# The last FFN of a hybrid block: instructions in a written order on every engine, two tiles ahead, and one more group in seven block products

## The chip, the cores and the metric

The kernel runs on one core of a Trainium2 chip. The metric is the device time of one execution in microseconds (us). Of the kernel before three runs were timed: 1880.12, 1881.79 and 1884.59, median 1881.79.

The engines are named as in the profile: PE is TensorE (matmul), DVE is VectorE, ACT is ScalarE, POOL is GpSimd and SP is SyncE, on which most DMAs are issued.

## The reference

One block over 256 tokens of 2048 channels, in float32: an FFN (SwiGLU), a mixer (mLSTM heads beside an RG-LRU), and a second FFN, each with a residual and a layer norm, and each modulated by shift, scale and gate that come from a vector c ("adaLN"). What matters here is the second, the last FFN:

```python
def _swiglu(u, w13, w2):
    g, v = jnp.split(u @ w13, 2, axis=-1)
    return (jax.nn.silu(g) * v) @ w2
...
mod = (jax.nn.silu(c) @ w_ada[l] + b_ada[l]).reshape(B, N_SUBLAYERS, 3, D_MODEL)
...
y = _swiglu(modulate(x, 2), ffn2_w13[l], ffn2_w2[l])
x = _layer_norm(ALPHA * x + FFN_WEIGHT * gate[:, 2, None, :] * y, ln_g[l, 2], ln_b[l, 2])
```

w13 is 2048 x 11264 (5632 gate columns g and 5632 value columns v), w2 is 5632 x 2048.

## The kernel before

**Products in halves.** Each float32 weight tile (128 x 2048, 1 MB) is loaded by a DMA on SP and split in two float32r halves: ACT casts the high half (`split`, L108), DVE subtracts it from the tile for the low half (L110). A product of a tile with 128 tokens is 12 matmuls of 512 columns: for each of four row blocks high by high, low weight by high, and high weight by low token half (`mov_t`). A tile that multiplies both token tiles (256 tokens) takes 24. Raw tiles have four buffers, high and low halves three each.

**Groups.** The last FFN goes through the 5632 columns in 11 groups of 512, called 0 to 10. For each group it makes g and v, then silu(g) * v as a 128 x 512 tile for each token tile, turns that by four transposes on PE (tile `th`, `turn_one`, L814), and ACT and DVE make its high and low half (`hth`, L816, and `htl`, L817). The w2 products of a pair of groups are added over the pair and then into `yacc` (L743, L745). Such a w2 product of one tile with both token tiles is called an X step below; the X steps of a pair run in the two groups behind it, four in each, two for a block of 512 output columns: the first with the pair's even group, the second with its odd one.

**Plain and fast groups.** Groups 0, 1 and 10 are plain (`rows_block`): eight tiles, 192 matmuls. Groups 2 to 9 are fast (`fast_block`): on half of the columns the 2 x 2 block product is done with seven block products in place of eight, P1 to P7 in the words of this text, each 12 matmuls, with sums of the weight tiles that DVE makes in place, and sums of the tokens (`sums`) that are made once. The other tiles of a fast group are two G (gate) and two V (value), 24 matmuls each. A fast group thus has 7 x 12 + 4 x 24 = 180 matmuls, and 4 x 24 = 96 with its X steps: 276. In the trace of before the seven products' tiles are `hfw`/`lfw`: P1 is the tile with b0 (`lfw_50` in group 5), P5 `50p` (its weight is a subtraction at L756), P6 `50q` (L761), P3 `55`, P7 `54q` (L766), P2 `51`, P4 `51p` (L775). The banks are `fa` (P1, then P6 and P7), `fb` (P5 and P3), `fc` and `fd`. ACT copies each product out (`kept`, L730); DVE adds the finished sums (L780, L782, L792) and multiplies (L793).

**adaLN tiles.** Shift, scale and gate need one DVE instruction for each 1 MB tile of w_ada (`ada_tile`, L210). 16 of them, those for the last gate, are left when the last FFN begins; before, `tick` gives one for every second load.

**Ahead and behind.** Before group 2 the residual x is written to DRAM (tile `xd`), its place is used for the token sums, and `restore` reads it back behind group 9 (`x<-xd`, POOL) and scales it. `closing` does the X steps of the last three groups, called (n, k) for output block n and group 8 + k; `residual` (L334, L335) adds what is finished to x. The last block of columns has its weight tiles multiplied by the gate first (`gated`, L1035), and `boundary` ends the kernel with the residual and the layer norm.

**What sets the order.** PE's matmuls, and where `V`, `A`, `G`, `T` or `Q` stands in place of `nc.vector` and so on, are issued in the program's order on their engine ("pinned"). In the last FFN before only PE's matmuls are pinned; the splits, sums, copies, turns and additions on DVE and ACT, and the loads, are placed by a scheduler.

## Time and profile before

| | us |
|---|---|
| profiled execution | 1882.46 |
| its span, first to last instruction | 1880.7 |
| PE busy | 1861.4 |
| DVE busy | 1561.3 |
| ACT busy | 895.1 |
| POOL busy | 43.2 |
| last FFN, from about 1177 to the end | 703.7 |

The mean granted clock of TensorE is 0.998 of full speed. In the rows below a line begins with its start and its length in us (timeline), or with its line, engine, operation, output and inputs (groups); the number in brackets is the idle time of the engine ahead of it, and what ended it. Records of matmuls overlap: the distance of their starts is what one costs.

### The profile page before, as it was taken

The numbers are of one execution on the slowest core, as the hardware profiler recorded it, in microseconds if no ns is written. First come the engines' busy times: TensorE is split into PE (matmuls) and PEld (weight loads), VectorE is DVE, ScalarE is ACT, GpSimd is POOL, SyncE is SP. The second block draws the span as 40 slices with busy tenths as digits, with TensorE's granted clock in tenths as the row PEclk, the third lists the DMA queues.
The fourth block names the chain that finished last, engine by engine and source line by source line (L and its number), as shares of the span: only waits on it lengthen the run. The fifth ranks groups of instructions, "written<-read, shape, count | busy, mean of one in ns | idle before, by whom it ended". The sixth has DMA issues, their size and how long they took to land.

```text
span 1880.7 us, 21240 instructions
## 1 busy us (share of the span) xinstructions
PE 1861.4 (99%) x8495; PEld 1526.0 (81%) x8495; DVE 1561.3 (83%) x1467; ACT 895.1 (48%) x847; POOL 43.2 (2%) x68
## 2 busy tenths in 40 slices
PE   8999999999999999999999999999999999999998
PEld 5788888888888888788888887878778888888886
DVE  6899998887887987889997877789887788778776
ACT  4543444533334335756644356454544455545441
POOL 0000000000000000100000121000000000000000
PEclk9999999999999999999999999999999999999999
DMA  9989889999899987478687574768855654564662
GB/s 377 417 354 366 319 311 347 357 348 355 344 357 355 339 331 269 148 276 296 244 317 296 203 264 182 268 246 300 307 210 190 224 212 168 202 224 186 239 224 90
DMA packets 74931, 520.06 MB, mean 277 GB/s; under 512 B 8736, under 2 KB 8912, under 8 KB 13520
## 3 DMA queue, kind: packets, MB, share of 16 engines
q1 hardware_dynamic: 72144, 507.54, 71.6%
q0 software_dynamic: 960, 7.37, 1.0%
q10 hardware_dynamic: 1728, 3.80, 0.6%
q8 instruction: 66, 1.08, 0.2%
q14 instruction: 33, 0.27, 0.0%
HBM read 514.46 MB, written 4.22 MB: 276 GB/s over the span
## 4 chain that ended last, share of the span: by engine, by line
PE 92%; DVE 4%; DMA 2%; issue 1%; ACT 1%; POOL 0%; POOLq 0%; DVEq 0%; SPq 0%; ACTq 0%
PE py L133 9%; PE pj L281 5%; PE fa L133 5%; PE fb L133 4%; PE fc L133 3%; PE fd L133 3%; PE py L293 3%; PE py L294 3%; PE py L292 3%; PE pj L283 3%; PE fg L293 3%; PE fg L294 3%; PE fg L292 3%; PE fv L293 3%; PE fv L292 3%; PE fv L294 3%
## 5 line engine op out<-in xcount | busy, mean ns | idle before, releaser
L210 DVE CUSTOM_DVE_ANT_0 ada<-ada,scb,badac 128x2048 f32<-128x2048 f32 x110 | 258.0, 2345 | 39.5 <-DMA ada<-in_w_ada 39.0
L108 ACT CAST hw<-rw 128x2048 fp32r<-128x2048 f32 x81 | 155.1, 1914 | 218.0 <-DMA rw<-in_w 60.6
L110 DVE TENSOR_TENSOR lw<-rw,hw 128x2048 fp32r<-128x2048 f32 x81 | 185.1, 2287 | 55.8 <-ACT hw L108 55.0
L110 DVE TENSOR_TENSOR lfw<-rfw,hfw 128x2048 fp32r<-128x2048 f32 x48 | 109.9, 2289 | 17.2 <-ACT hfw L108 17.2
L281 PE MATMUL pj<-u,hs 128*128 128x512 f32 x512 | 122.5, 391 | 0.0
L108 ACT CAST hra<-rra 128x2048 fp32r<-128x2048 f32 x38 | 72.6, 1914 | 102.2 <-DMA rra<-in_w_r 43.1
L108 ACT CAST hfw<-rfw 128x2048 fp32r<-128x2048 f32 x48 | 91.9, 1915 | 47.8 <-PE py L133 28.2
L281 PEld LDWEIGHTS pj<-u,hs 128*128 128x128 f32 x512 | 94.3, 188 | 18.4
L133 PE MATMUL py<-lw,hth 128*128 128x512 f32 x256 | 99.8, 390 | 2.1 <-DVE lw L110 2.1
L133 PE MATMUL py<-hw,hth 128*128 128x512 f32 x256 | 100.4, 392 | 0.0
L293 PE MATMUL py<-lw,hth 128*128 128x512 f32 x256 | 99.8, 390 | 0.1
L294 PE MATMUL py<-hw,htl 128*128 128x512 f32 x256 | 99.7, 390 | 0.0
L133 PE MATMUL py<-hw,htl 128*128 128x512 f32 x256 | 99.7, 389 | 0.0
L292 PE MATMUL py<-hw,hth 128*128 128x512 f32 x256 | 97.3, 392 | 0.0
L108 ACT CAST hfg<-rfg 128x2048 fp32r<-128x2048 f32 x28 | 53.6, 1914 | 86.1 <-DMA rfg<-in_w 48.8
L108 ACT CAST hs<-rs 128x2048 fp32r<-128x2048 f32 x32 | 61.0, 1908 | 68.7 <-PE pj L281 53.6
L293 PE MATMUL fg<-lfg,u 128*128 128x512 f32 x224 | 87.4, 390 | 0.1
L294 PE MATMUL fg<-hfg,u 128*128 128x512 f32 x224 | 87.3, 390 | 0.0
L293 PE MATMUL fv<-lfv,u 128*128 128x512 f32 x224 | 87.2, 389 | 0.0
L294 PE MATMUL fv<-hfv,u 128*128 128x512 f32 x224 | 87.1, 389 | 0.0
L108 ACT CAST hfv<-rfv 128x2048 fp32r<-128x2048 f32 x28 | 53.6, 1913 | 66.7 <-DMA rfv<-in_w 41.3
L292 PE MATMUL fg<-hfg,u 128*128 128x512 f32 x224 | 84.5, 392 | 0.0
(727 smaller groups left out, 4764.4 us busy)
## 6 DMA issues: line engine op xcount, KB each, us to landing
ada<-in_w_ada SPq DMA_DIRECT2D x138, 1024.0 KB, 6.5
rw<-in_w SPq DMA_DIRECT2D x81, 1024.0 KB, 5.5
rfw<-in_w SPq DMA_DIRECT2D x50, 1024.0 KB, 4.8
rra<-in_w_r SPq DMA_DIRECT2D x45, 1024.0 KB, 7.4
rs<-in_w_s SPq DMA_DIRECT2D x32, 1024.0 KB, 5.0
rfg<-in_w SPq DMA_DIRECT2D x28, 1024.0 KB, 6.7
rfv<-in_w SPq DMA_DIRECT2D x28, 1024.0 KB, 5.5
rwo<-in_w_out SPq DMA_DIRECT2D x16, 1024.0 KB, 4.8
```

Of the source, the lines that this page charges most:

```text
L108: act.copy(cut(hi, w), like(raw[:, w], hi))
L110: low.tensor_sub(cut(lo, w), like(raw[:, w], lo), cut(hi, w).bitcast(F32))
L133: self.last = getattr(self.engine, op)(*args, **kw)
L210: vec.tensor_tensor_reduce(raw[:, c], raw[:, c], scb[:, c], 1.0, base, ALU.mult, ALU.add, to)
L281: nc.tensor.matmul(ps, hi[:, k * P:(k + 1) * P], both(k), start=k == 0, stop=False)
L283: nc.tensor.matmul(ps[:, 0:S], lo[:, k * P:(k + 1) * P], uh[:, k, :], start=False, stop=k == KT - 1)
L292: pe.matmul(o, acth[:, k0 + j, tk], cut(hi, w), start=first and j == 0, stop=False, **kw)
L293: pe.matmul(o, acth[:, k0 + j, tk], cut(lo, w), start=False, stop=False, **kw)
L294: end = pe.matmul(o, actl[:, k0 + j, tk], cut(hi, w), start=False, stop=last and j == 3, **kw)
```

## The change

A new function `last_ffn` takes the place of the branches in `ffn` that made the last FFN. It first writes a list of steps (a PE part, a preparation of its weight, and work behind it), and then issues them (`flow`), everything pinned: weight tiles are prepared as long as no more than AHEAD = 3 prepared tiles are held, the current one among them; the work behind a step is issued right behind its matmuls, and the products that some steps return ahead of the next preparations. `beside` places extra work behind given preparations: seven adaLN tiles, the scaling of x, its DMA to DRAM and the token sums in groups 0 and 1, and nine adaLN tiles behind every third preparation in groups 2 and 3.

The order of a group is a string: `P` and `G`/`V` as above, `X` an X step and `t` a turn. Groups 2 to 9 use S4, and group 10, which is now fast too, uses S2 with two of the closing's steps in it.

The residual isn't read back: `gated_sum` multiplies `yacc` by the gate (two times four 512-wide products behind two preparations of group 10), and a DMA on POOL adds the scaled x from DRAM into it. The gate's row is fetched four preparations ahead of group 10. P6's weight is made with a scalar_tensor_tensor, its sign turned, so that P4's is an addition. `gated` for the closing's first tile comes behind all its steps.

The core of the diff:

```diff
-    ffn(2, a["w13_2"], a["w2_2"], None)
+    last_ffn(2, a["w13_2"], a["w2_2"])
...
+AHEAD = 3
+S4 = "P1 t X t P5 X P6 P3 X P7 P2 G P4 G X V V"
+S2 = "P1 t G t P5 X P6 P3 G P7 P2 X P4 V V"
...
+        def flow():
+
+            hls, late, n, m = {}, [], 0, 0
+            for i, (pe, prep, after) in enumerate(steps):
+                for f in late:
+                    f()
+                while n < len(steps) and (n <= i or len(hls) < AHEAD):
+                    if steps[n][1]:
+                        hls[n] = steps[n][1]()
+                        for f in extras.get(m, ()):
+                            f()
+                        m += 1
+                    n += 1
+                pe(hls.pop(i, None))
+                late = after() or [] if after else []
...
+            def after():
+                b, t, ps = now.pop()
...
+                A.copy(hth[:, :, tk], ps)
+                V.tensor_sub(htl[:, :, tk], ps, hth[:, :, tk].bitcast(F32))
...
+                if w == "P5":
+                    W["c", q] = raw(q, 4, row_c)
+                    a, c = W["a", q], W["c", q]
+                    V.tensor_sub(a[0], c[0], a[0])
+                    hl = halves(a, "p")
...
+                if w == "P6":
+                    W["d", q] = raw(q, 5, q == 1)
+                    a, d = W["a", q], W["d", q]
+                    V.scalar_tensor_tensor(a[0], a[0], -1.0, d[0], op0=ALU.mult, op1=ALU.subtract)
+                    hl = halves(a, "q")
...
+        def gated_sum(t):
+            def go():
+                for n in range(4):
+                    c = slice(n * 512, (n + 1) * 512)
+                    V.tensor_mul(yacc[t][:, c], yacc[t][:, c], gate[:, c])
+                G.dma_start(yacc[t], xd[:, t, :], accum_op=ALU.add)
...
+        beside([scaled(0), scaled(1), ada, ada, ada, *sums(0, in_x), ada, ada])
+        first_group(nxt.pop())
+        plain_group(1)
+        beside([ada] * 9, 3, 3)
+        for b in range(2, n_b - 1, 2):
...
+                for i in range(2):
+                    fast_group(b + i, 1, xs, S4, b > 2 and not DOUBLE)
...
+        beside([lambda: gate_rows(s, 0.5)], -4)
+        beside([gated_sum(0), gated_sum(1)], 4, 2)
...
+            for n, k in ((0, 0), (0, 1), (1, 0), (1, 1), (0, 2), (1, 2), (2, 0), (2, 1), (2, 2)):
...
+        flow()
+        fine[0] = True
+        gated(0)
```

Where it moves instructions. DVE at the head of group 6, before: `lfw_60p` and `lfw_60q` are the low halves for P5 and P6, L756 and L761 the subtractions that make their weights, `lw_4_0` and `lw_5_0` the low halves of the X steps, `htl` the low halves of the turned tokens, L792 and L793 the former group's last additions and products.

```order
L110 TENSOR_TENSOR lfw_60_10592<-fw_10589,hfw_60_10591 128x2048
L756 TENSOR_TENSOR fw_10589<-fw_10616,fw_10589 128x2048
L792 TENSOR_TENSOR fv_10321<-fv_10321,fb_10182 128x512
L766 TENSOR_TENSOR fw_10616<-rfw_65_10676,fw_10616 128x2048
L793 TENSOR_TENSOR fs_10208<-fs_10208,fv_10321 128x512
L110 TENSOR_TENSOR lw_4_0_10623<-rw_4_0_10620,hw_4_0_10622 128x2048
L792 TENSOR_TENSOR ft_10268<-ft_10268,fa_10181 128x512
L110 TENSOR_TENSOR lfw_60p<-fw_10589,hfw_60p 128x2048
```

The same place on DVE now; every pinned instruction has one line number, that of the helper that issues it. `f_...` are the sums of the products, `ht` the turned tokens.

```order
L142 TENSOR_TENSOR f_10332<-f_10332,f_10269 128x512
L142 TENSOR_TENSOR f_10282<-f_10282,f_10200 128x512
L142 TENSOR_TENSOR f_10213<-f_10213,f_10332 128x512
L142 TENSOR_TENSOR f_10401<-f_10401,f_10282 128x512
L142 TENSOR_TENSOR fw_60_10536<-fw_64_10600,fw_60_10536 128x2048
L142 TENSOR_TENSOR lfw_60p<-fw_60_10536,hfw_60p 128x2048
L142 TENSOR_TENSOR lw_5_0_10625<-rw_5_0_10622,hw_5_0_10624 128x2048
L142 TENSOR_TENSOR ht_10628<-th_10629,ht_10628 128x4x128
L142 SCALAR_TENSOR_TENSOR fw_60_10536<-fw_60_10536,rfw_65_10662 128x2048
L142 TENSOR_TENSOR lfw_60q<-fw_60_10536,hfw_60q 128x2048
L142 TENSOR_TENSOR ht_10628<-th_10669,ht_10628 128x4x128
```

The subtraction for P5 has moved from ahead of the former group's last additions to behind them and both products. The scalar_tensor_tensor for P6 stands between the two turns' low halves, and the second of these behind `lfw_60q`.

ACT at the same place, before: `hfw_60q` is P6's high half, `hth` the high half of the turned tokens.

```order
L108 CAST hfw_60p<-fw_10589 128x2048
L108 CAST hw_5_0_10680<-rw_5_0_10678 128x2048
L816 CAST hth_10175<-th_10607 128x4x128
L730 COPY fs_10614<-fa_10587 128x512
L816 CAST hth_10175<-th_10650 128x4x128
L108 CAST hfw_60q<-fw_10589 128x2048
L730 COPY ft_10674<-fb_10588 128x512
```

And now:

```order
L142 CAST hfw_60p<-fw_60_10536 128x2048
L142 COPY f_10620<-f_10607 128x512
L142 CAST hw_5_0_10624<-rw_5_0_10622 128x2048
L142 CAST ht_10628<-th_10629 128x4x128
L142 CAST hfw_60q<-fw_60_10536 128x2048
L142 CAST ht_10628<-th_10669 128x4x128
L142 COPY f_10689<-f_10676 128x512
```

The cast of the second turn (`ht_...<-th_...`, its second row) has moved behind the cast of `hfw_60q`.

DVE in the middle of group 3, with the adaLN tiles (ISA rows), now; `lfw_30q` is P6's low half, `lfw_34q` P7's, and the rows ahead of them make their weights.

```order
L142 ISA ada_9395,adac<-ada_9395,scb,badac 128x2048
L142 ISA adac 128x1
L142 TENSOR_TENSOR ht_9398<-th_9399,ht_9398 128x4x128
L142 SCALAR_TENSOR_TENSOR fw_30_9300<-fw_30_9300,rfw_35_9432 128x2048
L142 TENSOR_TENSOR lfw_30q<-fw_30_9300,hfw_30q 128x2048
L142 TENSOR_TENSOR ht_9398<-th_9439,ht_9398 128x4x128
L142 TENSOR_TENSOR lfw_35_9462<-rfw_35_9432,hfw_35_9461 128x2048
L142 TENSOR_TENSOR lw_0_3_9494<-rw_0_3_9491,hw_0_3_9493 128x2048
L142 ISA ada_9497,adac<-ada_9497,scb,badac 128x2048
L142 ISA adac 128x1
L142 TENSOR_TENSOR rfw_34_9367<-rfw_34_9367,rfw_35_9432 128x2048
L142 TENSOR_TENSOR lfw_34q<-rfw_34_9367,hfw_34q 128x2048
```

Before, the scheduler placed such tiles, as in group 2 ahead of `lfw_20q`:

```order
L761 TENSOR_TENSOR fw_8922<-rfw_25_9015,fw_8922 128x2048
L817 TENSOR_TENSOR htl_8629<-th_8989,hth_8628 128x4x128
L210 ISA ada_9140,adac<-ada_9140,scb,badac 128x2048
L210 ISA adac 128x1
L110 TENSOR_TENSOR lfw_20q<-fw_8922,hfw_20q 128x2048
```

One stands now ahead of the combination for P6 and the next ahead of that for P7.

## The prediction

> **What bounds the kernel now.** I read the page first, for which engine is full; then the stages of the last FFN (1177 us to the end) as windows; then what TensorE (PE) waited for there; then the timeline around the longest wait and at the start of a steady group. The page:

> ```profile
> span 1880.7 us, 21240 instructions
> PE 1861.4 (99%) x8495; PEld 1526.0 (81%) x8495; DVE 1561.3 (83%) x1467; ACT 895.1 (48%) x847; POOL 43.2 (2%) x68
> ```

> PE is the bound. The profiled execution took 1882.46 us (span 1880.7 and 1.76 around it), 0.67 above the median of 1881.79. Windows: the last FFN's first two groups with the head of group 2, then groups 2 to 4, then four steady groups (from group 5), in columns length, PE, PEld, DVE, ACT, POOL, granted clock, DMA share, GB/s:

> ```profile
> 1177.00:1300.00 123.00, 120.42 (x531) 98.87 (x530) 105.09 (x71) 60.79 (x45) 0.00 (x0) 0.99 0.76 282
> 1300.00:1436.40 136.40, 134.09 (x595) 109.70 (x594) 114.88 (x73) 69.97 (x52) 0.00 (x0) 1.00 0.68 254
> 1436.40:1690.30 253.90, 253.90 (x1137) 210.32 (x1137) 201.86 (x125) 131.03 (x92) 0.00 (x0) 1.00 0.55 199
> ```

> In the steady groups PE is never idle: 253.9 / 4 = 63.5 us each, with DVE (VectorE) busy for 201.86 / 4 = 50.5 of it. DVE thus has 13 us a group, and whether they suffice depends on its order. What PE waited for in the last FFN:

> ```profile
> PE fa L133 <- DVE lfw_20q L110: 2.6, 1, 2.6
> PE py L133 <- DVE lw L110: 2.1, 2, 1.3
> PE th L814 <- DVE fu L793: 0.2, 1, 0.2
> ```

> All three wait for DVE, 4.9 us in sum. The longest, from both sides:

> ```profile
> 1260.05 0.39 PE L133 MATMUL fa<-hfw_20q,ws 128*128 128x512 f32 x1
> 1263.02 0.50 PE L133 MATMUL fa<-lfw_20q,ws 128*128 128x512 f32 x1 [2.58 <-DVE lfw_20q L110]
> 1258.40 2.35 DVE L210 CUSTOM_DVE_ANT_0 ada<-ada,scb,badac 128x2048 f32<-128x2048 f32 x1 [2.08 <-DMA ada<-in_w_ada]
> 1260.68 2.29 DVE L110 TENSOR_TENSOR lfw_20q<-fw,hfw_20q 128x2048 fp32r<-128x2048 f32 x1
> ```

> An adaLN tile stood ahead of the low half of P6's weight (lfw_20q), 2.28 us from start to start, and PE stood still. Keep this place in mind: the change writes such an order by hand.

> **Prices.** Steady groups, the cost of each kind of work, and group 5's head on DVE, ACT (ScalarE) and PE:

> ```profile
> L110 DVE TENSOR_TENSOR lfw<-rfw,hfw 128x2048 fp32r<-128x2048 f32 x24 | 55.0, 2291 | 10.2 <-ACT hfw L108 10.2
> L108 ACT CAST hfw<-rfw 128x2048 fp32r<-128x2048 f32 x24 | 46.0, 1915 | 20.1 <-PE py L133 14.1 <-PE fd L133 3.2 <-PE fb L133 1.3
> L816 ACT CAST hth<-th 128x512 fp32r<-128x512 f32 x8 | 4.6, 579 | 13.7 <-PE th L814 13.7
> L133 DVE SCALAR_TENSOR_TENSOR x<-x,mvp,ln_g 128x512 f32<-128x512 f32 x6 | 4.2, 748 | 0.1
> L781 ACT ACTIVATE fs<-fs 128x512 f32<-128x512 f32 x8 | 5.0, 630 | 17.7 <-DVE fs L780 17.7
> ```

> ```profile
> 1435.29 2.29 DVE L756 TENSOR_TENSOR fw<-fw,fw 128x2048 f32<-128x2048 f32 x1
> 1437.50 0.68 DVE L792 TENSOR_TENSOR fv<-fv,fb 128x512 f32<-128x512 f32 x1
> 1438.10 2.28 DVE L766 TENSOR_TENSOR fw<-rfw,fw 128x2048 f32<-128x2048 f32 x1
> 1448.94 2.29 DVE L761 TENSOR_TENSOR fw<-rfw,fw 128x2048 f32<-128x2048 f32 x1
> 1451.14 1.28 DVE L817 TENSOR_TENSOR htl<-th,hth 128x512 fp32r<-128x512 f32 x2
> 1453.35 2.29 DVE L110 TENSOR_TENSOR lfw_50q<-fw,hfw_50q 128x2048 fp32r<-128x2048 f32 x1 [0.93 <-ACT hfw_50q L108]
> 1450.92 0.59 ACT L816 CAST hth<-th 128x512 fp32r<-128x512 f32 x1 [3.42 <-PE th L814]
> 1451.40 1.92 ACT L108 CAST hfw_50q<-fw 128x2048 fp32r<-128x2048 f32 x1
> 1436.44 0.39 PE L133 MATMUL fa<-lfw,u 128*128 128x512 f32 x1
> 1437.12 0.39 PE L133 MATMUL fa<-lfw,u 128*128 128x512 f32 x1
> 1444.38 0.60 PE L814 MATMUL th<-ident,fs 128*128 128x128 f32 x4
> 1445.05 0.39 PE L133 MATMUL py<-lw,hth 128*128 128x512 f32 x1
> ```

> From start to start: a 2048-wide DVE operation 2.2 us (1435.29 to 1437.50), a 512-wide one 0.6 (to 1438.10); cast to low half 1.95 (1451.40 to 1453.35); a matmul 0.68 / 3 = 0.227, so a product of 12 is 2.72, an X step of 24 is 5.44, four transposes 0.45 (1444.38 to 1445.05, less one matmul). A group of 276 matmuls and two turns is 276 x 0.227 + 0.9 = 63.5, as the window has it. A subtraction to the cast that reads it I take at 2.4 (2.29 and a hand-over), the scalar_tensor_tensor of P6 at 2.4 too: 2.2 if it streams like a subtraction, at most 4 x 0.75 = 3.0 by the 512-wide row.

> **Part by part.** (a) Group 10 in seven products: 12 matmuls fewer, 12 x 0.227 = **-2.7**. (b) The waits above go with their order: **-4.9**; and **-1.7** of slow clock, shown under (g).

> (c) The steady group, t = 0 where PE ends the former group's last V step. PE runs P1 (2.72), a turn, X1 (5.44), a turn, P5, X2, P6, P3, X3, P7 and so on. Now DVE. The subtraction for P5 stands behind the former group's two additions of finished sums and two products; the last addition needs the last V matmul, so 0.2 + 3 x 0.6 puts the subtraction at 2.0. (Before, L756 ran at 1435.29, ahead of that end.) Cast 4.4, low half 6.3 to 8.5, X2's low half behind its cast to 10.8, the first turn's low half to 11.4, P6's scalar_tensor_tensor 11.4, cast 13.9, low half 15.8 to 18.0, the second turn's low half 18.1 to 18.7. On ACT the second turn's cast stands behind P6's: 13.9 + 1.8 = 15.7, ready at 16.3. (Before, it ran first, at 1450.92.)

> Even groups (4, 6, 8): X2 multiplies by the tokens just turned. PE starts X2 at 2.72 + 0.45 + 5.44 + 0.45 + 2.72 = 11.8, does the first token tile until 14.5, waits for the second's high part until 16.3, runs two matmuls, waits for its low part until 18.75: 1.8 + 2.0 = 3.8 us. PE is then late enough for all that follows. 3 x 3.8 = **+11.3**.

> Odd groups (5, 7, 9): X2 uses older tokens and ends at 17.2. P6's second matmul (17.5) waits for the low half at 18.07: 0.6 to 0.7. P3's low half follows the turn's (18.7 to 20.9): 0.1. X3's follows two additions, about 1.2: ready 24.3 against 23.7, 0.7. P7's addition, cast and low half chain 2.3 + 2.0 + 2.2 behind that: 30.9 against 29.8, 1.1. Sum 2.6; 3 x 2.6 = **+7.7**.

> (d) Nine adaLN tiles lie in groups 2 and 3, behind every third prepared tile. By the order each group has three of them right ahead of P6's, P7's and P4's combination, where no slack is left, at 2.28 each: 3.8 + 6.8 = 10.6 in group 2, 2.6 + 6.8 = 9.4 in group 3, **+20.0**. The wait of 2.58 above is the same thing happening once. The seven tiles and the sums in groups 0 and 1 I cost at nothing: there 11 preparations of 2.2, 7 x 2.28 and some 10 us of sums make 50 us of DVE work under 12 X-sized steps of PE (65 us). With that cover gone they cost up to 4.

> (e) Group 10 has the odd group's start (P6 0.7) and two sets of four 512-wide products with the gate, 4 x 0.6 = 2.4 each, one ahead of P3 (0.1 + 2.4 = 2.5), one ahead of P7's addition (1.1 + 2.4, less 0.6 of X3's additions: 2.9). V1 follows P4 with one product of cover; ACT's Silu of 0.63 waits for an addition behind P4's low half and holds V1's cast: 0.6 + 0.6 + 2.0 + 2.2 - 2.7 = 2.7. Sum **+8.8**. Of the DMAs, the weight loads on SP now go in the order of the preparations, with four raw buffers and some 4 us a preparation, so about 12 us ahead; gate's row starts on POOL four preparations ahead of group 10, and the accumulating DMA that replaces two reads of x is first needed some 30 us later. By their landing times I cost them at nothing, hidden behind those preparations; each that isn't costs up to its row:

> ```profile
> rfw<-in_w SPq DMA_DIRECT2D x50, 1024.0 KB, 4.8
> x<-xd POOLq DMA_DIRECT2D x2, 1024.0 KB, 7.4
> gate<-rowd POOLq DMA_DIRECT2D x1, 1024.0 KB, 8.3
> ```

> (f) Closing: (0,2) needs both turns of group 10. DVE has the low halves of (0,2) and (1,2) ahead, the latter not before 7.4 since its buffer holds (1,0) until 5.4, then four gate products, a cast and a low half: 7.4 + 2.2 + 2.4 + 2.0 + 2.2 + 0.6 puts the first turn's low part at 16.8 against PE's 11.8, 5.0 in two parts. (2,2): six operations on x (3.6) lie ahead of its low half, some 2.2 of them covered, 1.4. gated(0) now stands behind the additions that wait for (2,2) itself: 2.1 of additions and statistics, then 4 x 0.6, then a low piece: 5.1. Sum **+11.5**. In the tail, token tile 1's first matmuls go ahead of tile 0's end while that is awaited: up to 12 x 0.227, half taken, **+1.4**.

> (g) The clock behind a gap. Windows behind the 2.58 us gap:

> ```profile
> 1263.00:1264.00 1.00, 0.98 (x4) 0.84 (x5) 1.00 (x1) 0.00 (x0) 0.00 (x0) 0.96 0.95 401
> 1264.00:1265.00 1.00, 1.00 (x3) 0.73 (x3) 1.00 (x1) 0.00 (x0) 0.00 (x0) 0.50 0.91 385
> 1266.00:1267.00 1.00, 1.00 (x4) 0.81 (x3) 1.00 (x1) 0.00 (x0) 0.00 (x0) 0.50 0.90 147
> 1267.00:1268.00 1.00, 1.00 (x5) 0.77 (x5) 0.37 (x1) 0.60 (x2) 0.00 (x0) 0.84 0.83 344
> ```

> Three us at half clock, about 1.7 us lost (the 1.7 of (b)); the gaps of the py row, at most 1.3, show none. The even groups' waits (3.8 with 0.5 of work in them), five in groups 2, 3 and 10 and two in the closing are long enough. In groups 2, 3 and 10 a late PE only shortens its next wait for DVE; elsewhere it costs 3 x 1.7 + 2 x 1.7 = 8.5, of which I take **+8**.

> [...]

> Sum: -2.7 - 4.9 - 1.7 + 11.3 + 7.7 + 20.0 + 8.8 + 11.5 + 1.4 + 8 = +59.4, 1941.9 for the profiled execution, **1941** at the median's level.

> **Rivals.** *Full cover (faster):* two tiles prepared ahead give DVE 5.4 to 8 us of lead, and PE stays the bound. For it: 13 us of free DVE time a group, and no idle PE in four groups before. Against: the row order. It decides at one point, whether the second turn's low part is there by 14.5 and P6's by 17.3; then -9.3, 1873.

> *Shorter chain:* every wait is 1 us less than I count, because hand-overs and the scalar_tensor_tensor are at their low ends. Even 2.8, odd 0.1, groups 2 and 3 14.0, group 10 4.9, closing 8.5, no tail: 36.1 - 9.3 + 5 of clock = +32, 1914; without the clock 1909.

> *Clock holds in the steady groups:* if the two parts of an even group's wait (1.8 and 2.0) are each too short for a dip, as the 1.3 of the py row was, only the closing's two pay 1.7 each: 3.4 in place of 8, 1937. [...]

> *Clock dips paid in full:* 14 waits of 2 us or more, each with 1.7 not absorbed, 24 in place of 8: 1957. For it: DVE and ACT also wait on PE for buffers, so a late PE can delay the preparations that follow.

> *No change:* the order's slack is as it was and only ends move: 1882.

> **Chances.** Forecast 0.44, shorter chain 0.20, full dips 0.17, clock holds 0.07, full cover 0.09, no change 0.03. A measurement of this kernel can tell about 0.2% (3.8 us) from no change. Faster by more: 0.09; within: 0.03; slower: 0.88. The range leaves out full cover, no change and 0.08 at the outer ends: from 1900 (the shorter chain at 1909, with the closing half as long and the tail's turn worth nothing) to 1962 (full dips and 4 us in groups 0 and 1).

> **What would show it.** Right: in groups 5 to 9 the P1 to P1 distance alternates, about 67 (69 with a clock dip) and 66 against 63.5; PE waits in X2 of even groups for the turned tokens first on ACT, then DVE; groups 2 and 3 last about 74 and 73; PE waits for gated(0)'s low half after (2,2). Wrong: 63.5 in every group, the second turn's cast not behind P6's, or PE's waits naming DMA.

## The result, and the profile after

The changed kernel takes 1946.82 us (median of 4 runs, 1944.03 to 1948.28) against 1881.82: a ratio of 1.0342, 95% interval 1.0324 to 1.036. 1941 was forecast, slower by 59; it is slower by 65. The profiled execution took 1947.58, with a span of 1945.8 and a mean granted clock of 0.985 (0.998 before).

The page, after:

```profile
span 1945.8 us, 21240 instructions
PE 1889.3 (97%) x8483; PEld 1536.3 (79%) x8483; DVE 1572.6 (81%) x1470; ACT 898.3 (46%) x854; POOL 43.8 (2%) x68
```

PE has 12 matmuls fewer and is busy for 28 us more, since its matmuls last longer where the clock is lower: at half clock in group 6 they start 0.43 us apart (1549.46 to 1549.89), ahead of it 0.23. That is 24 us of it, worked out below. All of the 65 us lie in the last FFN. Windows from the start of P1 to that of the next P1, groups 2 to 9, then group 10 with its two X steps, then the closing; the columns are as in the prediction:

```profile
1242.32:1317.93 75.61, 69.38 (x285) 55.37 (x284) 57.68 (x35) 34.30 (x27) 0.00 (x0) 0.93 0.61 236
1317.93:1391.91 73.98, 68.12 (x286) 54.64 (x285) 56.70 (x35) 34.08 (x27) 0.00 (x0) 0.95 0.59 227
1391.91:1460.98 69.07, 65.77 (x286) 53.49 (x285) 50.27 (x31) 32.52 (x23) 0.00 (x0) 0.98 0.48 183
1460.98:1527.17 66.19, 64.56 (x286) 52.22 (x285) 50.00 (x31) 32.32 (x23) 0.00 (x0) 1.00 0.50 191
1527.17:1597.23 70.06, 66.77 (x286) 54.20 (x285) 50.27 (x31) 32.52 (x23) 0.00 (x0) 0.95 0.47 180
1597.23:1663.39 66.16, 64.51 (x286) 52.20 (x284) 50.00 (x31) 32.31 (x23) 0.00 (x0) 1.00 0.50 191
1663.39:1733.59 70.20, 66.91 (x286) 54.30 (x284) 50.27 (x31) 32.52 (x23) 0.00 (x0) 0.95 0.47 180
1733.59:1799.87 66.28, 64.63 (x287) 52.29 (x286) 50.08 (x31) 32.48 (x24) 1.09 (x2) 1.00 0.50 190
1799.87:1863.07 63.20, 57.47 (x238) 45.48 (x236) 47.84 (x33) 28.34 (x21) 1.79 (x2) 0.95 0.61 200
1863.07:1945.80 82.73, 65.43 (x257) 50.25 (x255) 54.67 (x68) 17.03 (x15) 3.38 (x4) 0.91 0.33 114
```

DVE does the same 50 us of work in a steady group as before (50.5). Its order is another. Odd groups take 66.2 at full clock, even ones 69 to 70 with slow clock in them. What PE waited for in the last FFN (the first rows):

```profile
PE py L142 <- ACT ht L142: 9.7, 5, 2.8
PE py L142 <- DVE ht L142: 8.8, 6, 1.7
PE tl L301 <- ACT hw22l L142: 3.6, 1, 3.6
PE f L142 <- DVE lfw L142: 2.1, 1, 2.1
PE py L142 <- DVE lw L142: 2.0, 4, 0.8
```

The turned tokens (`ht`) come first, on ACT and then on DVE, and the closing's tile 0 (`hw22l`) next. Group 6 shows the place, as timelines of PE, DVE and ACT:

```profile
1541.47 0.39 PE L142 MATMUL py<-hw,ht 128*128 128x512 f32 x1
1543.44 0.50 PE L142 MATMUL py<-hw,ht 128*128 128x512 f32 x1 [1.59 <-ACT ht L142]
1545.88 1.22 PE L142 MATMUL py<-hw,ht 128*128 128x512 f32 x2 [1.71 <-DVE ht L142]
```

```profile
1529.17 2.28 DVE L142 TENSOR_TENSOR fw<-fw,fw 128x2048 f32<-128x2048 f32 x1
1533.51 2.29 DVE L142 TENSOR_TENSOR lfw_60p<-fw,hfw_60p 128x2048 fp32r<-128x2048 f32 x1 [2.05 <-ACT hfw_60p L142]
1538.61 2.28 DVE L142 SCALAR_TENSOR_TENSOR fw<-fw,rfw 128x2048 f32<-128x2048 f32 x1
1542.94 2.29 DVE L142 TENSOR_TENSOR lfw_60q<-fw,hfw_60q 128x2048 fp32r<-128x2048 f32 x1 [2.04 <-ACT hfw_60q L142]
1545.15 0.68 DVE L142 TENSOR_TENSOR ht<-th,ht 128x512 fp32r<-128x512 f32 x1
```

```profile
1541.01 1.90 ACT L142 CAST hfw_60q<-fw 128x2048 fp32r<-128x2048 f32 x1 [4.76 <-DVE fw L142]
1542.81 0.58 ACT L142 CAST ht<-th 128x512 fp32r<-128x512 f32 x1
```

With t = 0 at 1527.2 the chain runs as it was worked out: the subtraction for P5 at 2.0, P6's sum at 11.4, its cast at 13.8 and the second turn's cast right behind, the low half at 15.8, the second turn's at 18.0. The scalar_tensor_tensor takes what a subtraction does, 2.28. In the second wait the clock falls to half, and it stays there behind it (such a stretch is called a dip below):

```profile
1544.00:1545.00 1.00, 0.18 (x1) 0.00 (x0) 1.00 (x1) 1.00 (x1) 0.00 (x0) 0.76 0.00 0
1547.00:1548.00 1.00, 1.00 (x4) 0.81 (x3) 1.00 (x2) 0.00 (x0) 0.00 (x0) 0.50 0.00 0
1551.00:1552.00 1.00, 1.00 (x5) 0.77 (x5) 0.24 (x1) 1.00 (x1) 0.00 (x0) 0.83 0.00 0
```

From 1544.5 to 1551.3 it is at 0.5. The time lost to it is (1 - clock) x PE busy in windows of one us: summed over the last FFN up to 1934 that is 24.1 us, and 1.7 before the change.

### The profile page after: what moved, and what is told of

Its sections match the earlier page's. It is cut to its first block, busy times and chain, and to the rows that moved or that the text cites. A ratio compares the mean times of both kernels' runs of the same rounds, so it can differ in the third digit from the quotient of the medians.

```text
span 1945.8 us, 21240 instructions
## 1 busy us (share of the span) xinstructions
PE 1889.3 (97%) x8483; PEld 1536.3 (79%) x8483; DVE 1572.6 (81%) x1470; ACT 898.3 (46%) x854; POOL 43.8 (2%) x68
## 4 chain that ended last, share of the span: by engine, by line
PE 77%; DVE 12%; ACT 5%; issue 4%; DMA 1%; POOL 0%; DVEq 0%; POOLq 0%; ACTq 0%; SPq 0%
PE f L142 15%; PE pj L290 5%; PE py L142 5%; PE py L302 3%; PE py L301 3%; PE py L303 3%; PE pj L292 3%; DVE fw L142 3%; PE fg L302 2%; PE fg L303 2%; PE fg L301 2%; PE fv L303 2%; PE fv L301 2%; PE fv L302 2%; PE rv L765 2%
## 5 line engine op out<-in xcount | busy, mean ns | idle before, releaser
L142 PE MATMUL py<-hw,ht 128*128 128x512 f32 x656 | 218.9, 406 | 18.4 <-ACT ht L142 9.7
L142 PEld LDWEIGHTS py<-hw,ht 128*128 128x128 f32 x656 | 127.4, 195 | 49.1 <-ACT ht L142 11.6
L142 PE MATMUL py<-lw,ht 128*128 128x512 f32 x328 | 131.8, 402 | 2.0 <-DVE lw L142 2.0
L117 ACT CAST hw<-rw 128x2048 fp32r<-128x2048 f32 x40 | 76.6, 1914 | 94.3 <-DMA rw<-in_w 59.6
L117 ACT CAST hra<-rra 128x2048 fp32r<-128x2048 f32 x38 | 72.6, 1915 | 102.4 <-DMA rra<-in_w_r 46.3
L142 DVE CUSTOM_DVE_ANT_0 ada<-ada,scb,badac 128x2048 f32<-128x2048 f32 (+1 forms) x50 | 110.8, 2217 | 3.0 <-DMA ada<-in_w_ada 2.8
L302 PE MATMUL py<-lw,hth 128*128 128x512 f32 x256 | 99.8, 390 | 0.1
L303 PE MATMUL py<-hw,htl 128*128 128x512 f32 x256 | 99.7, 389 | 0.0
L301 PE MATMUL py<-hw,hth 128*128 128x512 f32 x256 | 97.3, 392 | 0.0
L119 DVE TENSOR_TENSOR ls<-rs,hs 128x2048 fp32r<-128x2048 f32 x32 | 73.0, 2281 | 11.0 <-ACT hs L117 11.0
L142 PEld LDWEIGHTS py<-lw,ht 128*128 128x128 f32 x328 | 63.8, 194 | 16.8 <-DVE lw L142 3.6
L142 DVE TENSOR_TENSOR lra<-rra,hra 128x2048 fp32r<-128x2048 f32 x29 | 66.3, 2287 | 8.8 <-ACT hra L142 6.7
L292 PE MATMUL pj<-u,ls 128*128 128x256 f32 x512 | 66.4, 283 | 0.0
## 6 DMA issues: line engine op xcount, KB each, us to landing
ada<-in_w_ada SPq DMA_DIRECT2D x138, 1024.0 KB, 6.8
rw<-in_w SPq DMA_DIRECT2D x81, 1024.0 KB, 6.1
rra<-in_w_r SPq DMA_DIRECT2D x45, 1024.0 KB, 7.4
rs<-in_w_s SPq DMA_DIRECT2D x32, 1024.0 KB, 5.1
rfg<-in_w SPq DMA_DIRECT2D x24, 1024.0 KB, 6.2
rfv<-in_w SPq DMA_DIRECT2D x24, 1024.0 KB, 6.0
rfw<-in_w SPq DMA_DIRECT2D x21, 1024.0 KB, 7.0
rwo<-in_w_out SPq DMA_DIRECT2D x16, 1024.0 KB, 4.8
```

What stands on the lines that cost most here:

```text
L117: act.copy(cut(hi, w), like(raw[:, w], hi))
L119: low.tensor_sub(cut(lo, w), like(raw[:, w], lo), cut(hi, w).bitcast(F32))
L142: self.last = getattr(self.engine, op)(*args, **kw)
L292: nc.tensor.matmul(ps[:, 0:S], lo[:, k * P:(k + 1) * P], uh[:, k, :], start=False, stop=k == KT - 1)
L301: pe.matmul(o, acth[:, k0 + j, tk], cut(hi, w), start=first and j == 0, stop=False, **kw)
L302: pe.matmul(o, acth[:, k0 + j, tk], cut(lo, w), start=False, stop=False, **kw)
```

## The experiments

The theory: nothing is short but the order, and each displaced instruction costs its own wait. Rivals: two tiles ahead are too few in any order; DVE has too much to do; group 10 in seven products costs it. Each run starts from the changed kernel and has one edit, but for the four at the end, under "All of it". The kernel before was timed again beside each set of runs, with medians of 1882.1 to 1885.0 us, and most of the single edits were timed twice. So a difference of 3 us from the changed kernel's 1946.82 says little, and what an edit is worth is best read from the stage that it touches.

**Turned tokens first.** Their copy and low half are issued ahead of the next preparations:

```diff
                 for f in late:
                     f()
+                if not prep:
+                    pe(None)
+                    late = after() or []
                 while n < len(steps) and (n <= i or len(hls) < AHEAD):
```

> Edit: the copy and the low half of a turned token tile are issued ahead of the next preparations, not behind them; nothing else moves. Theory (the written order on DVE and ACT makes the waits): the even groups 4, 6 and 8 (69.1, 70.1 and 70.2 us now) lose their wait in X2 and the slow clock behind it and come to about 66, like the odd ones; group 2 loses about 4 us, the closing's wait for group 10's tokens (4.5 us and some 3 us of slow clock) nearly goes. Sum about -24: 1923 us, between 1912 and 1934. Rival (depth: with two tiles ahead PE outruns the preparations whatever their order): the waits only move from X2 to the next steps, 1940 or more.

1929.59 us, 17 less. The four steady groups from 5 to 8 in one window:

```profile
1455.18:1719.72 264.54, 257.55 (x1137) 209.12 (x1136) 200.01 (x124) 129.66 (x92) 0.00 (x0) 1.00 0.50 191
```

66.1 each at full clock, even and odd alike, as expected. What is left there is P6 and P7:

```profile
PE f L142 <- DVE lfw_60q L142: 1.0, 1, 1.0
PE f L142 <- DVE lfw_64q L142: 0.8, 1, 0.8
```

So the wait for the tokens is gone, with 1.8 us a group left at P6 and P7 (the odd groups had 1.6 in all before this edit), and depth isn't its cause. The gain is 7 us short of the 24: group 2 stays at 72.7, since adaLN tiles now hold P6, P7 and P4 there, and the closing waits for the second turn behind a gated tile still.

**Sums one preparation earlier.** The DVE sums for P5 (groups 4 to 9), P6, P7 and P4 move up by one preparation, for P5:

```diff
-                    W["a", q] = raw(q, 0, q == 0)
-                    return halves(W["a", q])
+                    W["a", q] = a = raw(q, 0, q == 0)
+                    hl = halves(a)
+                    if row_c:
+                        W["c", q] = c = raw(q, 4, True)
+                        V.tensor_sub(a[0], c[0], a[0])
+                    return hl
```

> Edit: the DVE sums that make the weights of P5, P6, P7 and P4 are issued one preparation earlier, ahead of the additions that wait for PE (P5's only from group 4 to 9, where its tile has room); buffers and depth are as they are. Theory (order): groups 4 to 9 come to 63.5 to 64 us each (69.1, 66.2, 70.1, 66.2, 70.2, 66.3 now), 27 us less; groups 2, 3 and 10 some 12 less in sum. 1908 us, between 1898 and 1920. Rival (depth): the steady groups stay above 65, 1938 or more.

1898.39 us, 48 less, the most of all edits that keep a written order. Four steady groups:

```profile
1440.50:1694.47 253.97, 253.97 (x1138) 210.44 (x1137) 202.10 (x124) 131.10 (x92) 0.00 (x0) 1.00 0.53 199
```

254 us, PE never idle, as before the change (253.9), with the same buffers and two tiles ahead. This settles the rivals of depth and of DVE's work for these groups. The run lies just inside the expected 1898 to 1920: groups 2 and 3 gave 15 us (67.9 and 66.4 now) and group 10 with its X steps 7 (55.8), where 12 had been expected of the three.

**adaLN tiles elsewhere.** Four of nine to groups 0 and 1, five to the ends of groups 2 and 3:

```diff
+        beside([ada] * 4, 2)
...
-        beside([ada] * 9, 3, 3)
+        for at in (11, 14, 25, 26, 29):
+            beside([ada], at)
```

> Edit: of the nine adaLN tiles in groups 2 and 3, four go to groups 0 and 1, five to the ends of groups 2 and 3 (behind the preparations of G, X or V there), none ahead of the sums for P6, P7 and P4. Theory (each tile ahead of a sum costs its 2.3 us and often a slow clock): group 2 falls from 75.6 to about 70, group 3 from 74.0 to about 67, groups 0 and 1 stay: 1935 us, between 1930 and 1940. Rival (DVE has too little time there whatever the order, groups 0 and 1 have no room): 1944 to 1952.

1938.02 us, 9 less, but of two runs that lie 8 us apart (1934.0 and 1942.0; the profile is of the slower). Groups 0 and 1, then 2, then 3:

```profile
1177.00:1250.68 73.68, 69.02 (x304) 55.63 (x302) 67.51 (x54) 34.98 (x25) 0.65 (x1) 1.00 0.89 356
1250.68:1318.90 68.22, 65.98 (x286) 53.43 (x285) 51.10 (x30) 34.43 (x27) 0.00 (x0) 0.97 0.58 216
1318.90:1386.19 67.29, 64.59 (x286) 52.17 (x285) 54.25 (x33) 34.08 (x27) 0.00 (x0) 1.00 0.56 220
```

Groups 2 and 3 lose 7.4 and 6.7 us, as the theory says. Groups 0 and 1 end 8.4 us later than in the changed kernel (65.3 to the same point), of which 2.2 lie ahead of them, so the four tiles cost 6 there: both theories are right in one place each. The cover there was enough for seven tiles and not for eleven.

**DVE and ACT free.** The same program with the scheduler placing DVE's and ACT's instructions in the last FFN:

```diff
     def last_ffn(s, w13, w2):
+        V, A = nc.vector, nc.scalar
```

> Edit: in the last FFN the instructions of DVE and ACT are no longer held in the written order (the scheduler places them, as before the change); PE's matmuls, the loads, buffers, group 10 in seven products and x added from DRAM are as changed. Theory (order): nearly all of the loss goes, steady groups 63.5, and the 12 matmuls of group 10 remain saved: about 1880 us, between 1868 and 1895. Rival (depth, or the new group 10 and closing): it stays above 1920.

1885.27 us; ratio to the kernel before 1.0006, interval 0.9996 to 1.0016. So the written order on DVE and ACT is the whole loss, and the rest of the change, with seven products in group 10 and x added from DRAM, comes to no loss and no gain. Two waits are there that the kernel before doesn't have, 5.4 us together against the 2.7 of the 12 matmuls:

```profile
1171.86 1.21 PE L142 MATMUL f<-hf,u 128*128 128x512 f32 x4 [1.94 <-DVE u L142]
1831.76 1.22 PE L142 MATMUL py<-hw,ht 128*128 128x512 f32 x2 [3.42 <-DVE ht L1010]
```

An adaLN tile of the last FFN got in on DVE ahead of the mixer's last operands (the first row), and the closing waited for the turned tokens (the second).

**The clock.** In the even groups' wait PE does small matmuls that nobody reads, 12 in each of two places, then 6:

```diff
+                hold = bank(f"hold{kg}")
+                idle(hold, 12)
+                mov_t(pss[n][1], hl, *hts[kg], 0, 1, False, last, T, gap=lambda: idle(hold, 12))
```

> Edit: in the X step that follows the turns in groups 2, 4, 6 and 8, PE does 24 more small matmuls (128 columns, into a bank that nobody reads), 12 ahead of the second token tile and 12 ahead of its first matmul with the tokens' low half. All waits stay; PE is only not idle in them. Theory (behind such a wait the clock is halved for 3 to 7 us): groups 4, 6 and 8 fall from 69.1, 70.1 and 70.2 us to about 67, group 2 by up to 3: 1937 us, between 1933 and 1942. Rival (the time beyond the waits is something else, not the clock): 1946 or more, since PE does more.

1942.14 us: 5 less with more work on PE, but groups 4, 6 and 8 at 69.0 and not 67. Each small matmul leaves two records in the trace, about 0.11 us apart, so a place took 2.6 us and outran its wait. With 6:

> Edit: as in the run with small matmuls in the even groups' wait, with half of them, since the 24 records of 0.108 us in each place lasted 2.6 us and outran the waits of some 1.8 (groups 4, 6 and 8 came to 69.0 with the clock at 1.00 throughout). Now 1.3 us in each. Theory (slow clock is the rest of those groups' loss): the waits end as in the changed kernel, the clock holds, groups 4, 6 and 8 take 67.1 us each (69.1, 70.1, 70.2 in the changed kernel): 1939 us, between 1935 and 1942. Rival (the waits are the whole loss): 1945 or more.

1939.17 us, 7.7 less than the changed kernel. Group 6 from P1 to P1, and its wait:

```profile
1524.16:1591.67 67.51, 66.89 (x310) 55.28 (x308) 50.10 (x31) 32.51 (x23) 0.00 (x0) 1.00 0.49 187
```

```profile
1538.69 1.50 PE L142 MATMUL hold<-ident 128*128 128x128 f32 x12
1540.43 0.50 PE L142 MATMUL py<-hw,ht 128*128 128x512 f32 x1 [0.24 <-ACT ht L142]
1541.01 1.50 PE L142 MATMUL hold<-ident 128*128 128x128 f32 x12
1542.88 0.74 PE L142 MATMUL py<-hw,ht 128*128 128x512 f32 x2 [0.38 <-DVE ht L142]
```

The waits end where they did, the clock is 1.00, and the group takes 67.5 in place of 70.1, as do groups 4 and 8. The slow clock by itself was 2.6 us there, and useless work took it away. A dip can also be missing by chance, as the next run shows, but not this often: without the small matmuls groups 4, 6 and 8 had one in 10 of 12 cases (the changed kernel and the runs on adaLN tiles, group 10 and the closing), with them the waits in groups 2, 4, 6 and 8 of both runs had none in 8.

**Group 10 plain**, in the written order:

```diff
-        fast_group(n_b - 1, 1, es, S2, False)
+        plain_group(n_b - 1)
+        for _ in range(2):
+            next(es)()
```

> Edit: group 10 is plain again (8 products, 12 matmuls more, no sums of weights), in the written order; the rest as changed. Theory (the seven products' sums, copies and Silu cost more in waits and slow clock there than 2.7 us): group 10's loss of some 10 us against its matmuls falls to 3 or less: 1942 us, between 1937 and 1946. Rival (the 12 matmuls are saved in full): 1949.5.

1935.97 us, 11 less, with 12 matmuls more. The same stretch, group 10 with two X steps:

```profile
1794.65:1849.98 55.33, 55.33 (x249) 45.83 (x248) 32.11 (x25) 21.17 (x14) 1.79 (x2) 1.00 0.74 229
```

55.3 us for 240 matmuls without a wait, against 63.2 for 228 in the changed kernel, 7.9 less. The theory holds and was too timid: the plain group waits for nothing. The rest is not the plain group's. Group 10 starts 5.2 us earlier in this profile than in that of the changed kernel, though nothing ahead of it was edited: dips were missing there. Group 6 had the same two waits (1.59 and 1.71 in the changed kernel), no dip, and took 67.5 us in place of 70.1:

```profile
1541.81 0.50 PE L142 MATMUL py<-hw,ht 128*128 128x512 f32 x1 [1.58 <-ACT ht L142]
1544.25 0.73 PE L142 MATMUL py<-hw,ht 128*128 128x512 f32 x2 [1.72 <-DVE ht L142]
```

```profile
1525.53:1593.01 67.48, 64.18 (x285) 52.28 (x284) 50.09 (x31) 32.52 (x23) 0.00 (x0) 1.00 0.49 187
```

**The closing.** The gated tiles of the closing one or two preparations later, tile 0 ahead of the last additions, and used last:

```diff
-        beside([lambda: gated(1, half(0)), lambda: gated(2, half(1))], -4, 2)
+        beside([lambda: gated(1, half(0)), lambda: gated(2, half(1))], -2)
+        step(lambda _: None, lambda: gated(0))
...
-            for i in range(3):
+            for i in (1, 2, 0):
```

> Edit: in the closing the three tiles that are multiplied by the gate are prepared later or earlier: the first two behind the last two steps' tiles and so behind group 10's turned tokens, the third ahead of the additions of step (2,2), and the last block takes it last. Theory: the wait for the tokens (4.5 us and 3 of slow clock) falls to about 1, the wait for the third tile (4 us and 3 of slow clock) goes: 1935 us, between 1930 and 1941. Rival (DVE has too much to do there in any order): 1944 to 1950.

1934.45 us, 12 less. By the profiles the closing is worth 9.9 of it (72.9 us in place of 82.7); group 10 also starts 3.6 us earlier, by dips that were missing in groups that the edit doesn't touch. PE's waits from the closing's start are now two:

```profile
PE tz L142 <- ACT dm L142: 5.7, 1, 5.7
PE py L142 <- DVE ht L142: 1.3, 1, 1.3
```

The waits for the tokens and for tile 0 have gone, but the tail has one of 5.7 in place of 1.9: with tile 0 last, the scheduler (these matmuls are not in written order) ran the two token tiles' products interleaved, so that the first norm can't run beside the second tile's matmuls.

**All of it.** The early sums, the tokens first, the closing, the adaLN tiles one preparation later, and group 10's gate products behind P2 and the last V:

> Edit: the sums for P5, P6, P7 and P4 one preparation earlier, turned tokens ahead of the next preparations, the closing's gated tiles as in the run on the closing, adaLN tiles one preparation later (behind P6, P7, P4, V), and the gate products of group 10 behind P2 and the last V. Theory (order is all): against the run with early sums alone (1898.4) groups 2 and 3 give 4, group 10 1.5, the closing 12: 1880 us, between 1873 and 1889, so level with or better than the kernel before. Rival (some of the waits only move): 1890 or more.

1888.22 us, ratio 1.0024 (1.0014 to 1.0035): at the edge of the range, and the tail is why, with a wait of 6.9 in place of before's 0.8. Then the last block in written order too, the closing's gate products one preparation ahead of their halves, and one adaLN tile off the head of group 3:

> Edit: on top of the run with all reorderings (1888.2, where the last block's products of the two token tiles ran interleaved, so that DVE's tail of 18 us had both norms in it against 10.6 before): these 72 matmuls in written order, token tile 0 first; the gate products of the closing's tiles one preparation ahead of their halves; the nine adaLN tiles off the head of group 3. Theory (only order was lost): the tail gives back 7 us, groups 2 and 3 some 3: 1877 us, between 1870 and 1883, about 5 us less than the kernel before (12 matmuls fewer are 2.7 of it, the waits and slow clock of its groups 2 to 4 the rest). Rival (DVE's work in the closing is the bound in any order): 1884 or more.

1879.75 us, ratio 0.9973, interval 0.9963 to 0.9984: better than both kernels, by 0.27% than the one before. All of PE's waits behind 1240 are

```profile
PE py L142 <- DVE lw L142: 5.0, 6, 1.6
PE tz L142 <- ACT dm L142: 0.8, 1, 0.8
```

and the clock never falls in groups 2 to 10. So it was order, in this case with the closing's DVE work fitting as well. On this base, group 10 plain again (with its gate products back where the changed kernel has them):

> Edit: the kernel of the run with everything reordered, with group 10 plain (12 matmuls more, no sums). Theory: with the order mended the seven products save their matmuls: 2 to 3.5 us more than that run. Rival (as in the written order, the seven products cost more than they save there): less than that run by 1 us or more.

1879.76 us: no difference, neither as expected (2 to 3.5 more) nor as the rival had it (1 or more less). Group 10 and two X steps, with seven products and then plain, each in its own run:

```profile
1756.36:1811.53 55.17, 53.20 (x237) 43.42 (x236) 46.37 (x32) 28.61 (x21) 1.79 (x2) 1.00 0.65 207
```

```profile
1756.28:1811.62 55.34, 55.34 (x250) 45.83 (x249) 32.20 (x25) 21.20 (x14) 1.79 (x2) 1.00 0.74 229
```

The 12 matmuls (2.7 us) are saved and given back in PE idle time (55.17 against 53.20 busy): DVE has 46 us of work there in place of 32, and PE waits for it twice (1.6 and 0.4). And one tile ahead:

> Edit: the kernel of the run with everything reordered, with one tile prepared ahead in place of two (AHEAD = 2). Theory: a preparation takes cast and low half, 4.2 us, and the products of 12 matmuls 2.7, so P6 to P3 and P7 to P2 stall again in every group, by 2 us or more twice a group: 1910 us or more, which says that depth matters below two and order above. Rival (depth is nothing, order all): 1885 or less.

1975.59 us: PE waits 38.9 us in 27 places for an X step's low half alone. The stalls lie at X steps and at G tiles, one step behind P3 and P2, where the theory had put them. So depth does matter below two tiles, and with two it isn't what was missing.

## Why the prediction was right, point by point

The direction, the places and the size of each stage came out; the split between waiting and slow clock did not.

| Step | forecast | measured |
|---|---|---|
| odd groups 5, 7, 9 (above 63.5) | 2.6 each | 2.7, 2.7, 2.8 |
| even groups 4, 6, 8 | 3.8 and 1.7 of clock | 5.6, 6.6, 6.7 |
| groups 2 and 3 | 10.6, 9.4 | 12.1, 10.5 |
| group 10 with two X steps (above 52.6) | 8.8 | 10.6 |
| closing and tail (above 66.4, the best run's) | 12.9 and 3.4 of clock | 16.3 |

Here 63.5 and 52.6 are the times of 276 and of 228 matmuls with two turns at the prediction's prices, and 66.4 is the closing in the run with everything reordered.

(c) holds to the instruction: two links set the wait, the subtraction for P5 behind the last V and the second turn behind P6's cast. Undoing the second alone took away the even groups' extra, undoing the first with its like took away everything in the steady groups. The points at which full cover was to decide (the turn's low part at 14.5, P6's at 17.3) were missed at 18.6 and 18.0.

(d) The adaLN tiles cost PE time ahead of P6, P7 and P4; with all nine moved off those places, groups 2 and 3 fall by 14, and groups 0 and 1, which took four, rise by 6. That seven tiles in groups 0 and 1 are covered held, PE is busy throughout:

```profile
1177.00:1242.32 65.32, 65.32 (x294) 54.09 (x292) 56.59 (x42) 32.92 (x23) 0.65 (x1) 1.00 0.87 348
```

(e), (f) hold in their places; the plain group and the run on the closing show them as two separate sources, 7.9 and 9.9 us by their stages.

(a) is where the forecast counted a saving that nothing shows: it was entered as -2.7, which the stage only has if PE doesn't wait there. In the best order found, the seven products are worth 0.2 us in that stage and nothing in the total.

(g) is the mis-sized term. Taken were 8 us, as what is left of some 24 when a late PE shortens its next waits; the windows show 24.1 lost. That this is the 24 of the rival with dips paid in full is luck: the rival had 14 dips of 1.7, and there are 11, of which five lost 2.5 to 3.0. A dip was taken as the one before, 3.4 us at half clock, and those of groups 6 and 8, the first of group 2 and the two of the closing are twice that, which that one could not show. So groups 4, 6 and 8 paid 1.6, 2.6 and 2.7 above the 67.5 that such a group takes without a dip, and the closing 5.2, in place of 1.7 for each dip.

The waits err the other way. The recorded ones are shorter than forecast, 43.9 us (49.5 with 0.16 for each of 35 gaps, by which a matmul's record, 0.39 us long, outlasts its turn of 0.23) in place of 60.7, most of all in groups 2, 3 and 10, because a slow PE arrives later at the next wait. Group 3 shows it: in the run with group 10 plain, where it had no dip, its waits were 7.1 us in place of 5.9 and it took 72.4 in place of 74.0, so that of 3.4 us of slow clock 1.6 were paid. The assumption that a late PE shortens its next wait was right in kind; in groups 2, 3 and 10 it did not absorb all of it.

The sum of waits and clock was 68.7 by the forecast and is 76.6 by the stages (3.0 of it in neither the waits nor the windows); it is nearer than its two parts, since the clock is 16 above what was taken and the waits 11 below. The kernel before lost 8.2 by the same measure, not 6.6 (its waits in the prediction leave out one of 0.8 for ACT in the tail), so the total came out 6 us above the forecast. One reading in the prediction was loose, without effect on the sum: its first window, to 1300, holds not the head of group 2 but nearly all of it, since P1 of group 2 starts at 1242.80 and that of group 3 at 1305.61.

## What to carry to other kernels

Two tiles of lead are worth only what the order of the preparing engine makes of them: an instruction that waits for PE (a sum of finished products) must not stand ahead of one that PE waits for, and a sum that makes an operand belongs one preparation earlier than its cast. When an order is written by hand, compare it with the one a scheduler found at the places with the least slack, and let the scheduler place the same instructions once, to learn whether the order or the work is at fault. Before saving matmuls, ask whether the engine that feeds them has the time for the extra sums: here 12 matmuls bought 14 us of DVE work and no time. And read what an edit is worth from the stage that it touches: here dips came and went in stages that an edit had left alone, by 3.6 and 5.2 us a run.

## What the runs showed of the hardware

The length of a wait did not decide alone. In the first run under "All of it" one of 2.09 us had no dip behind it; the clock there:

```profile
1324.00:1327.40 3.40, 3.15 (x14) 2.60 (x15) 3.40 (x4) 1.98 (x2) 0.00 (x0) 1.00 0.00 0
```

And the two waits of groups 4, 6 and 8 (1.6 and 1.7, with 0.5 us of matmuls between) had no dip, one of 3.4 or one of 6.8 behind them in the changed kernel and the runs on group 10 and on the closing, whose written order is the same up to group 9. The group then took 67.5, 69.1 or 70.0 to 70.2 us. What decides between them no run here shows, so it stays open.
